# Modulation of four early chunks by row sums on VectorE, and a first group of four feature tiles as two groups of two

## The chip, the cores and the metric

The kernel runs on one core of one Trainium2 chip. The metric is device time in microseconds (us), the median of several runs of the whole program. All arrays are fp32 in HBM. To keep fp32 accuracy, the large products split each operand into a high part (rounded to the matmul's type, fp32r) and a low part (the rest), and sum three products: high x high, high x low, low x high.

## The reference, cut to what matters

One layer of an encoder, with 256 tokens and 2048 features. The conditioning vector c yields six vectors of 2048 (shift, scale and gate for each of two sub-layers). The change touches only the first shift and scale and the QKV projection that uses them.

```python
c_act = jax.nn.silu(c)
mod = c_act @ mod_w[i] + mod_b[i]
sh_m, sc_m, g_m, sh_f, sc_f, g_f = jnp.split(mod, 6, axis=-1)
hmix = x * (1.0 + sc_m[:, None, :]) + sh_m[:, None, :]
y = windowed_gqa_sink(hmix, positions, w_qkv, b_qkv, sink, w_o, b_o)   # proj = h @ w_qkv + b_qkv, width 3072
x = layer_norm(alpha * x + (1.0 + g_m[:, None, :]) * y, ln_mix_g[i], ln_mix_b[i])
hff = x * (1.0 + sc_f[:, None, :]) + sh_f[:, None, :]
y = sq_relu_mlp(hff, w1, b1, w2, b2)                                   # 2048 -> 8192 -> 2048
x = layer_norm(alpha * x + (1.0 + g_f[:, None, :]) * y, ln_mlp_g[i], ln_mlp_b[i])
```

## The kernel before

**Feature tiles and groups.** The 2048 features are 16 tiles of 128 (k = 0 to 15). QKV needs all of them as its contraction. The kernel cannot touch tile k before its shift and scale are known, and these are sums over all 2048 entries of c. So it takes the tiles in groups (`MIXG`, L32): 1, 1, 2, 4, 4, 4. For each group it streams the columns of `mod_w` that yield the group's scale and shift (array `modm`, two chunks for each tile), and then the rows of `w_qkv` for those tiles. Everything comes in chunks of 1 MiB, [128, 2048] fp32.

**The stream.** Class `Stream` (L174) holds the order of all chunks in `S.q`, as `plan` put them there. `loads` (L196) issues a load on the SP queue (L202) whenever one of the raw buffers is free: five, and three more (`MORE`) in the early part, out of memory that later serves as `gen2`. Entries of `S.side` are extra loads (parts of x) at fixed places of the order. `pump` (L223) goes through the chunks in this order. A weight chunk is cast in two halves to its high part on ScalarE (L247), and `low` (L214) makes the low part on VectorE (L218). A modulation chunk calls its `step`, if the pump was allowed that many (`vecs`); otherwise the pump stops there. The pump is called at the start of each weight chunk (`main`, L253) and after each half of it (`done`, L264), with `S.pace` modulation steps at most. While `S.pin` is set, what it issues keeps its place in its engine's program order; otherwise the tile framework may place it. With `S.behind`, a step's first matmul is put behind the latest matmul of the main work.

**Modulation.** Class `Mod` (L285): for most chunks `step` makes 16 small products on TensorE, c as a 32-wide stationary operand and the chunk as moving operand, four side by side (`quad`, L304; L307), accumulated in PSUM over the whole group. For listed chunks (`dve`) it multiplies by c on VectorE instead (L343 for the first, L345 after) into a partial sum that a last product folds in. Then the sum is copied to a row (L361), and `columns` (L365) turns the row into one value per partition through TensorE (L370, L377), and adds bias and 1 (L371 to L384). `modulated(g)` (L512) applies scale and shift to each tile of the group: high part on ScalarE (L519), product and low part on VectorE (L520, L521).

**QKV.** Output channels are six blocks of 512 (c). `qkv_first` (L542) does tiles 0 and 1, `qkv` (L563) the other groups, one weight chunk at a time: four (k, c) blocks, two token tiles, three products (`mm3`, L498 to L500), so 24 matmuls of 512 columns. `evict` (L526) then adds the two PSUM banks of a channel to its running sum on VectorE (L537), or copies them the first time on ScalarE (L535) after the bias product (L163). A pair in `CARRY` leaves its channel in PSUM for the next group. `ORDER` gives the order of a group's chunks; the six chunks in `LATE` are left for the attention stage. After the first chunk of the last group comes the rotary work (`rope`, L648 to L651), then attention, its projection, and the MLP.

**Start.** While the first chunks load, `idle(n)` (L597) keeps TensorE running with products of ones (L601).

## Time and profile before

| | us |
|---|---|
| median of 3 runs | 1095.23 |
| lowest, highest | 1093.78, 1096.64 |
| span of the profiled execution | 1098.2 |

The profiled execution is on record by its span alone, from its first instruction to its last. Engines: PE is TensorE's matmuls, PEld its weight loads, DVE VectorE, ACT ScalarE, POOL GpSimd, SP the engine that issues most loads. Busy shares over the span are 97% PE, 73% DVE, 48% ACT. A busy PE is not PE at its peak, since matmuls are pipelined and their ends are modelled. "L218" is line 218 of the kernel. In a row of a timeline or of the chain of waits, the first number is the start and the second the length. In a group's row stand the count, the total busy time, the mean in ns, and the idle time ahead of it with what ended it.

### The profile page before, as it was taken

What the parts mean: (1) busy time and instruction counts of PE and PEld (TensorE: products, weight loads), DVE (VectorE), ACT (ScalarE), POOL (GpSimd) and SP (SyncE); (2) the same over time, 40 slices, a digit from 0 to 9 for tenths busy, and PEclk for the clock granted to TensorE, in tenths of its full rate; (3) what the DMA queues carried; (4) which work ended last, traced back from release to release, by engine and by line L of the source; (5) the groups of instructions that cost most, each with busy time, mean ns of one, the idle gap of its engine ahead of it and who ended that gap; (6) DMA issues with size and microseconds to landing.
All of it is one profiled execution on the core that took longest, in us unless ns stands there. A gap on an engine that the chain in (4) does not pass through costs nothing.

```text
span 1098.2 us, 15487 instructions
## 1 busy us (share of the span) xinstructions
PE 1067.6 (97%) x6098; PEld 863.1 (79%) x6098; DVE 804.2 (73%) x1162; ACT 522.0 (48%) x806; POOL 30.0 (3%) x54
## 2 busy tenths in 40 slices
PE   8889999998999999999999999999999999999995
PEld 6657677665677799988888888888888888888884
DVE  4597899978899877754588889756666557665676
ACT  5333346765673537643344543344453334544340
POOL 1000000001000000000000010001000000000001
PEclk9989999999999999999999999999999999999998
DMA  9999987789985996555578788866555555557511
GB/s 384 425 427 425 427 357 280 271 297 379 377 315 201 361 360 244 185 192 192 195 301 303 272 313 306 312 220 225 184 189 190 197 196 186 178 185 267 191 75 77
DMA packets 43337, 292.70 MB, mean 267 GB/s; under 512 B 5104, under 2 KB 5232, under 8 KB 9472
## 3 DMA queue, kind: packets, MB, share of 16 engines
q1 hardware_dynamic: 39312, 279.85, 66.9%
q0 software_dynamic: 3200, 10.50, 2.7%
q10 hardware_dynamic: 752, 1.35, 0.3%
q8 instruction: 48, 0.79, 0.3%
q14 instruction: 25, 0.20, 0.0%
HBM read 289.57 MB, written 2.11 MB: 266 GB/s over the span
## 4 chain that ended last, share of the span: by engine, by line
PE 86%; DVE 7%; DMA 4%; ACT 2%; issue 1%; DVEq 0%; ACTq 0%
PE pa L995 16%; PE pa L500 15%; PE pa L498 15%; PE pa L499 15%; PE pa L996 8%; PE pa L972 3%; PE pa L971 3%; PE pa L973 3%; PE pm L307 3%; DVE wl L218 2%; DMA raw<-in_modm 2%; DMA raw<-in_modf 1%; DVE g L345 1%; DMA raw<-in_wqkv 1%; PE pa L687 1%; PE pa L743 1%
## 5 line engine op out<-in xcount | busy, mean ns | idle before, releaser
L218 DVE TENSOR_TENSOR wl<-raw,wh 128x1024 fp32r<-128x1024 f32 x332 | 403.9, 1223 | 223.6 <-ACT wh L247 222.9
L247 ACT CAST wh<-raw 128x1024 fp32r<-128x1024 f32 x332 | 347.1, 1051 | 441.3 <-PE pa L500 228.6
L498 PE MATMUL pa<-wh,g 128*128 128x512 f32 x816 | 324.1, 398 | 5.1 <-ACT g L519 2.6
L500 PE MATMUL pa<-wh,g 128*128 128x512 f32 x816 | 318.9, 392 | 4.1 <-DVE g L521 3.0
L499 PE MATMUL pa<-wl,g 128*128 128x512 f32 x816 | 320.0, 392 | 0.0
L995 PE MATMUL pa<-g,wh 128*128 128x512 f32 x768 | 270.1, 397 | 0.0
L996 PE MATMUL pa<-g,wl 128*128 128x256 f32 x768 | 214.9, 280 | 0.0
L498 PEld LDWEIGHTS pa<-wh,g 128*128 128x128 f32 x816 | 153.9, 189 | 46.8 <-issue 7.5
L500 PEld LDWEIGHTS pa<-wh,g 128*128 128x128 f32 x816 | 153.5, 188 | 41.2 <-DVE g L521 6.0
L499 PEld LDWEIGHTS pa<-wl,g 128*128 128x128 f32 x816 | 153.9, 189 | 33.0 <-issue 2.4
L995 PEld LDWEIGHTS pa<-g,wh 128*128 128x128 f32 x768 | 144.2, 188 | 36.0 <-issue 0.8
L996 PEld LDWEIGHTS pa<-g,wl 128*128 128x128 f32 x768 | 144.8, 189 | 0.1
L345 DVE SCALAR_TENSOR_TENSOR g<-raw,cact,g 128x1024 f32<-128x1024 f32 x65 | 82.6, 1280 | 2.8 <-DMA raw<-in_modf 2.3
L972 PE MATMUL pa<-g,wh 128*128 128x256 f32 x256 | 72.7, 285 | 0.4 <-DVE g L915 0.4
L971 PE MATMUL pa<-g,wh 128*128 128x256 f32 x256 | 72.5, 286 | 0.0
L973 PE MATMUL pa<-g,wl 128*128 128x256 f32 x256 | 72.3, 283 | 0.0
L307 PE MATMUL pm<-raw,cact 128*32 128x256 f32 (+2 forms) x776 | 48.8, 375 | 5.9 <-DMA raw<-in_modf 3.2
L971 PEld LDWEIGHTS pa<-g,wh 128*128 128x128 f32 x256 | 48.8, 192 | 1.3 <-issue 0.8
L972 PEld LDWEIGHTS pa<-g,wh 128*128 128x128 f32 x256 | 49.1, 192 | 0.9 <-DVE g L915 0.8
L973 PEld LDWEIGHTS pa<-g,wl 128*128 128x128 f32 x256 | 49.1, 192 | 0.0
L345 DVE SCALAR_TENSOR_TENSOR g4b<-raw,cact,g4b 128x1024 f32<-128x1024 f32 x32 | 40.7, 1280 | 9.0 <-DMA raw<-in_modgf 8.8
L307 PEld LDWEIGHTS pm<-raw,cact 128*32 128x32 f32 x776 | 20.9, 112 | 25.9 <-issue 11.5
(165 smaller groups left out, 741.6 us busy)
## 6 DMA issues: line engine op xcount, KB each, us to landing
raw<-in_w SPq DMA_DIRECT2D x64, 1024.0 KB, 4.9
raw<-in_w1b SPq DMA_DIRECT2D x48, 1024.0 KB, 5.0
raw<-in_modm SPq DMA_DIRECT2D x32, 1024.0 KB, 14.8
raw<-in_modf SPq DMA_DIRECT2D x32, 1024.0 KB, 6.9
raw<-in_wqkv SPq DMA_DIRECT2D x24, 1024.0 KB, 12.8
raw<-in_modgm SPq DMA_DIRECT2D x16, 1024.0 KB, 7.5
raw<-in_wo SPq DMA_DIRECT2D x16, 1024.0 KB, 7.5
raw<-in_w1a SPq DMA_DIRECT2D x16, 1024.0 KB, 7.6
```

Of the source, the lines that this page charges most:

```text
L218: self.pinned(nc.vector.tensor_sub(l, r, f32(self.hs[n])))
L247: self.pinned(nc.scalar.copy(h, s))
L307: i = nc.tensor.matmul(self.ps[32 * j:32 * j + 32, :w], lhsT[j] if type(lhsT) is list else lhsT, rhs[j], start=self.first, stop=stop)
L345: nc.vector.scalar_tensor_tensor(p[:, :e], s, cact[:, kt:kt + 1], p[:, :e], op0=OP.mult, op1=OP.add)
L498: nc.tensor.matmul(ps, xh, wh, start=start, stop=False)
L499: nc.tensor.matmul(ps, xh, wl, start=False, stop=False)
L500: S.prev = nc.tensor.matmul(ps, xl, wh, start=False, stop=stop).ins
L971: nc.tensor.matmul(o, wh(w, 128), hh, start=new, stop=False)
L972: nc.tensor.matmul(o, wh(w, 128), hl, start=False, stop=False)
L973: nc.tensor.matmul(o, wl(w, 128), hh, start=False, stop=end)
L995: nc.tensor.matmul(ps, wh(k, 128), hb, start=k == 0, stop=False)
L996: nc.tensor.matmul(ps[:, :256], wl(k, 128), hb[:, :256], start=False, stop=k == NK - 1)
```

## The change

1. `MIXG` becomes 1, 1, 2, 2, 2, 4, 4: tiles 4 to 7 are two groups of two, with eight modulation chunks in all as before, all of them now on TensorE (before, four of the eight on VectorE), and six weight chunks.
2. `MIXM` describes a new layout of `modm`: tiles 0 and 3 keep a pair of chunks for TensorE (`pair`), tiles 1 and 2 have a chunk with the 128 scale columns and one with the 128 shift columns, transposed, so that each partition holds one output feature and its 2048 weights. Class `Col` sums such a chunk along its row on VectorE, times c, with one `tensor_tensor_reduce` that starts from the bias. For that `broadcast_c` puts c into all partitions once (16 products and four copies on ScalarE).
3. `modulated` can take the tiles of a group one by one (used for tiles 2 and 3).
4. The planned order of chunks (`MODAT`), the carried channels and the place of the loads of x are set anew.
5. `S.steps` overrides the pace at single points; `STEPS` gives it for tiles 2 to 7 with `S.behind` set, and the steps of tiles 0 to 3 are called at named points of `run`. `ahead(nh)` casts up to nh halves in advance.
6. The fillers at the start become 7, 5 and 14 (before 16, 5 and 6).
7. The scratch tiles "t2" move from the small pool to a pool of their own that takes the memory of c's broadcast copy later.

```diff
-MIXG = (1, 1, 2, 4, 4, 4)
+MIXG = (1, 1, 2, 2, 2, 4, 4)
+MIXM = (1, 0, 0, 1, 2, 2, 4, 4)
...
+    cbp = early.enter_context(tc.tile_pool(name="cbp", bufs=1))
...
+            more.append(ctx.enter_context(tc.tile_pool(name="t2p", bufs=4)))
...
-            self.pump(self.pace, 2 * i + 2)
+            self.pump(self.steps.pop(0) if self.steps else self.pace, 2 * i + 2)
...
-                self.pump(self.pace)
+                self.pump(self.steps.pop(0) if self.steps else self.pace)
...
+    class Col:
+        def __init__(self, src, n, k):
+            self.src, self.n, self.k = src, n, k
+
+        def plan(self):
+            S.plan(self.src, self.step)
+
+        def step(self, raw):
+            d = (scm, shm)[self.n][:, self.k:self.k + 1]
+            S.pinned(nc.vector.tensor_tensor_reduce(out=raw, in0=raw, in1=cb, scale=1.0,
+                                                    scalar=modmb[:, self.n, self.k:self.k + 1],
+                                                    op0=OP.mult, op1=OP.add, accum_out=d))
+            if self.n == 0:
+                S.pinned(nc.vector.tensor_scalar_add(d, d, 1.0))
+
+    def broadcast_c():
+
+        cb = cbp.tile([128, D], F32, name="cb")
+        for q in range(4):
+            ps = psa.tile([128, 512], F32, name="pa")
+            for i in range(4):
+                nc.tensor.matmul(ps[:, i * 128:i * 128 + 128],
+                                 cact[:, 4 * q + i:4 * q + i + 1].to_broadcast([128, 128]), ident,
+                                 start=i == 0, stop=i == 3)
+            nc.scalar.copy(cb[:, q * 512:q * 512 + 512], ps)
+        return cb
...
-    m_mix = groups(a["modm"], MIXG, [(), (), (), (1, 3, 4, 6), (1, 3, 4, 6), (1, 3, 4, 6)])
+    pair = {k: Mod([a["modm"][2 * k + i] for i in range(2)], 64) for k in (0, 3)}
+    col = {(n, k): Col(a["modm"][2 * k + n], n, k) for n in range(2) for k in (1, 2)}
+    m_mix = [(pair[0], 0, 1), (None, 1, 1), (pair[3], 2, 2)]
+    m_mix += [(m, k0 + 4, nk) for m, k0, nk in groups(a["modm"][8:], MIXG[3:],
+                                                      [(), (), (1, 3, 4, 6), (1, 3, 4, 6)])]
...
-    LATE = [(4, 3), (5, 3), (4, 4), (5, 4), (4, 5), (5, 5)]
-
-    ORDER = {2: (1, 0, 2), 3: (5, 4, 3, 0, 2, 1), 4: (1, 2, 0), 5: (0, 1, 2)}
-    CARRY = {(LATE[n], LATE[n][1]) for n in (0, 2, 4)} | {((2, 2), 5), ((3, 1), 1), ((4, 0), 0), ((1, 2), 2)}
+    LATE = [(5, 3), (6, 3), (5, 4), (6, 4), (5, 5), (6, 5)]
+
+    ORDER = {2: (1, 0, 2), 3: (2, 0, 1), 4: (1, 2, 0), 5: (1, 2, 0), 6: (0, 1, 2)}
+    CARRY = {(LATE[n], LATE[n][1]) for n in (0, 2, 4)} | {((2, 2), 5), ((3, 1), 3), ((4, 0), 1), ((5, 0), 0), ((1, 2), 2)}
...
     m_mix[0][0].plan(2)
     S.plan(a["wqkv"][0])
-    m_mix[1][0].plan(2)
+    col[0, 1].plan()
+    col[1, 1].plan()
     S.plan(a["wqkv"][1])
+    S.side[len(S.q)] = lambda: load_x(1)
+    col[0, 2].plan()
     S.plan(a["wqkv"][2])
-
-    S.side[len(S.q)] = lambda: load_x(1)
-    m_mix[2][0].plan(3)
+    col[1, 2].plan()
+    pair[3].plan(2)
     wq(2, 1)
-    m_mix[2][0].plan(1)
+    MODAT = {2: (0, 4, 0), 3: (1, 2, 1), 4: (3, 3, 2), 5: (4, 4, 0)}
     for g in range(2, G):
-        n = len(ORDER[g])
-        if g + 1 < G:
-            S.side[len(S.q)] = lambda g=g: load_x(g)
-        for x, c in enumerate(ORDER[g][1:], 1):
+        if g > 3 and g + 1 < G:
+            S.side[len(S.q)] = lambda g=g: load_x(g - 1)
+        for x, c in enumerate(ORDER[g][1:]):
             if g + 1 < G:
-                m_mix[g + 1][0].plan([0, 0, 3][x] if g == 2 else [0, 2, 2, 2, 1, 1][x] if n == 6 else [0, 4, 4][x])
+                m_mix[g + 1][0].plan(MODAT[g][x])
             wq(g, c)
         if g == 2:
-            m_mix[3][0].plan(4)
+            S.side[len(S.q)] = lambda: load_x(2)
         if g + 1 < G:
+            m_mix[g + 1][0].plan(MODAT[g][2])
             wq(g + 1, ORDER[g + 1][0])
-        if g == 2:
-            m_mix[3][0].plan(1)
...
-    def modulated(g):
+    def modulated(g, ks=None):
         m, k0, nk = m_mix[g]
-        columns(m, modmb, (scm, shm), k0, nk)
-        hh, hl = g4(F32R), g4(F32R)
-        for k in range(nk):
+        ks = range(nk) if ks is None else ks
+        if m is not None and (k0 > 3 or k0 + ks[-1] in pair):
+            columns(m, modmb, (scm, shm), *((k0, nk) if k0 > 3 else (k0 + ks[-1], 1)))
+        if g not in held:
+            held[g] = g4(F32R), g4(F32R)
+        hh, hl = held[g]
+        for k in ks:
...
+    def ahead(nh):
+
+        S.nh = nh
+        S.pump(0)
+        S.nh = 5
+
     load_x(0)
     bq = bias_rows(a["bqkv"], QKV)
-    idle(16)
+    idle(7)
+    cb = broadcast_c()
     S.pin = True
     S.vecs(1)
     idle(5)
     S.vecs(1)
     modulated(0)
-    idle(6)
+    idle(14)
     msk = masks()
     S.nh, S.nl = 5, 4
-    S.pace = 1
-    run(qkv_first(0))
-    S.vecs(2)
-    run(qkv_first(1), [lambda: modulated(1)])
+    S.pace = 0
+    run(qkv_first(0), [lambda: S.vecs(2), lambda: ahead(2)])
+    run(qkv_first(1), [lambda: modulated(1), lambda: S.vecs(1), lambda: ahead(5)])
     trig = rotary_tables()
-    run(qkv_first(2))
-    S.vecs(4)
-    modulated(2)
+    run(qkv_first(2, [lambda: S.vecs(1)]), [lambda: S.vecs(1)])
+    modulated(2, [0])
+    S.vecs(1)
+    ahead(1)
+    modulated(2, [1])
     S.pace = VECS
+    STEPS = {(2, 1): (0, 0, 1), (2, 0): (0, 1, 1), (2, 2): (1, 0, 0),
+             (3, 2): (0, 1, 0), (3, 0): (0, 1, 1), (3, 1): (1, 0, 0)}
     S.pin = False
     for x, (g, c) in enumerate(qk_order):
         at = ORDER[g].index(c)
         mid = []
         if g < G - 1 and at == len(ORDER[g]) - 1:
             mid.append(lambda: modulated(g + 1))
+        S.steps = list(STEPS.get((g, c), ()))
+        S.behind = (g, c) in STEPS
         run(qkv(g, c), mid)
```

More of the change, by code (lines that the diff above doesn't have):

```diff
@@ L191, in __init__ @@
             self.side = {}
+            self.steps = []
         def plan(self, src, use=None, kept=0):
@@ L540, in banks, with qkv_first @@
         return [psa.tile([128, 512], F32, name="pa") for _ in range(NT)]
-    def qkv_first(n):
+    def qkv_first(n, then=()):
         wh, wl = S.main()
+        for f in then:
+            f()
         for i, (g, p) in enumerate(FIRST[n]):
@@ L1030, in hybrid_kernel @@
             if blk == 1:
-                gb = [sml.tile([128, 512], F32, name="gb", tag="t2", bufs=4) for _ in range(2)]
+                gb = [t2("gb") for _ in range(2)]
                 for n in range(2):
```

27 lines of the change are left out of this document (16 added, 11 removed).

## The prediction

> **What bounds the kernel now.** I began with the stretches of the span, because an average over 1098 us would hide that this kernel has stages with different limits.
>
> ```profile
> core 0: us, PE busy (x) PEld busy (x) DVE busy (x) ACT busy (x) POOL busy (x), PEclk, DMA share, GB/s
> 0.00:12.00 12.00, 9.95 (x88) 7.47 (x88) 5.31 (x20) 5.46 (x9) 4.96 (x16) 1.00 0.85 332
> 12.00:50.00 38.00, 32.82 (x319) 23.47 (x318) 17.42 (x28) 19.84 (x30) 0.00 (x0) 0.96 1.01 425
> 50.00:73.00 23.00, 21.77 (x134) 14.60 (x130) 22.96 (x31) 3.98 (x6) 1.01 (x2) 1.00 1.01 426
> 73.00:111.00 38.00, 35.61 (x183) 26.56 (x183) 29.04 (x36) 14.24 (x17) 0.90 (x1) 0.91 1.01 427
> 111.00:149.00 38.00, 35.56 (x208) 24.61 (x207) 32.92 (x48) 14.67 (x20) 0.00 (x0) 1.00 1.01 425
> 149.00:260.00 111.00, 109.75 (x605) 75.13 (x604) 101.98 (x195) 73.02 (x172) 4.25 (x8) 1.00 0.77 295
> 260.00:400.00 140.00, 136.34 (x938) 102.48 (x937) 121.71 (x231) 83.30 (x173) 3.96 (x6) 1.00 0.83 323
> 400.00:1098.00 698.00, 685.83 (x3639) 588.75 (x3637) 472.81 (x579) 307.49 (x384) 14.87 (x22) 0.99 0.60 218
> ```
>
> The row is: stretch, busy time of each engine with its instructions, granted clock, DMA share, rate. From 12 to 149 us the transfers never rest (share 1.01, 425 GB/s), so one 1 MiB chunk lands every 1.0486/0.426 = 2.46 us and no edit can bring data sooner. From 149 to 260 us the rate falls to 295 GB/s and VectorE is busy 102 of 111 us; after 400 us TensorE is busy 98%. Whatever the front gains or loses is therefore handed on to the end: behind it no transfer is short.
>
> TensorE's busy share says little in the front, so I counted matmuls. One 1 MiB chunk of QKV weights is four (k, c) blocks by two token tiles, hence 8 of the L500 kind (and 24 in all).
>
> ```profile
> 0.00:50.00 50.00, 9.53 (x24) 4.57 (x24) 0.97 0.97 402
> 50.00:73.00 23.00, 9.36 (x24) 4.48 (x24) 1.00 1.01 426
> 73.00:111.00 38.00, 16.83 (x43) 8.32 (x42) 0.91 1.01 427
> 111.00:149.00 38.00, 15.53 (x41) 7.36 (x41) 1.00 1.01 425
> ```
>
> By 73 us TensorE has done 48/8 = 6 chunks; eight have landed (counted below). Then come 43/8 = 5.4 chunks in 38 us. The chain of waits (start, length, what) says which limit acts when:
>
> ```profile
> 11.93 18.74 DMA raw<-in_modm
> ...
> 58.76 14.05 DMA raw<-in_wqkv
> 73.86 1.04 ACT wh L247
> 74.89 0.51 ACT g L519
> 75.45 0.79 PE pa L498
> ...
> 78.84 0.43 PE pa L500
> ...
> 82.79 0.23 PE pa L499
> ...
> 103.77 1.43 PE pm L307 x24
> ...
> 110.61 2.35 DVE wl L218 x2
> ...
> 129.13 1.48 PE pm L307 x24
> ...
> 130.90 0.87 ACT wh L247
> ...
> 134.84 1.22 DVE wl L218
> ...
> 139.12 2.36 DVE wl L218 x2
> ...
> 142.32 0.50 PE pa L500
> ```
>
> No transfer stands on the chain after 72.81 us. From 75 to 110 us it is TensorE working off the six chunks of feature tiles 4 to 7, which could not start before all eight modulation chunks of that group were in; then VectorE and ScalarE catch up with what had piled up. The first visible limit after the front is VectorE's rotary work:
>
> ```profile
> 66.66 0.61 PE L307 MATMUL pm<-g,onesf 128*32 128x256 f32 x8
> 148.50 0.69 DVE L537 TENSOR_TENSOR g<-g,pa 128x512 f32<-128x512 f32 x1 [0.68 <-PE pa L500]
> 149.22 0.69 DVE L648 TENSOR_TENSOR g<-g,trig 128x512 f32<-128x512 f32 x1
> ```
>
> **When chunks land.** The two DMA pieces of the chain end at 30.67 us (the tenth chunk, 10.25 MiB of the planned order with 0.25 of x) and at 72.81 us (27.25 MiB: the second weight chunk of the group of four): 42.14/17 = 2.48 us per MiB, which agrees with the rate. Counting on at 2.46 us, the last modulation chunk lands at 72.8 + 20.5 x 2.46 = 123.2 us, the third weight chunk of tiles 8 to 11 at 125.7, the first of tiles 12 to 15 at 128.1. TensorE takes that last modulation chunk only at 129.13: the front runs some 6 us behind its transfers.
>
> **The change, part by part.** From the first weight chunk of tiles 8 to 11 (38.25 MiB, 99.9 us) on, the planned order is the same as before, byte for byte. So the only thing to be won is the lateness.
>
> *Group of four as two groups.* In the new order the modulation of tiles 4, 5 is complete at 48.2 us (17.25 MiB), its weight chunks land at 54.4, 59.3 and 66.7; tiles 6, 7 are complete at 69.1, weights at 71.6, 82.6, 92.5; the last chunk of tiles 2, 3 lands ahead of them at 50.7. A chunk is 24 x 0.23 = 5.5 us of TensorE and begins about 2.6 us after landing (72.81 to 75.45). So tiles 2, 3 end at 50.7 + 2.6 + 5.5 = 58.8, and the six chunks run 58.8 to 64.3, to 69.8, to 75.3, to 80.8, then 85.2 to 90.7 and 95.1 to 100.6. The backlog is gone at about 101 us where it was worked off at 110.6. Tiles 8 to 11 then start when their last modulation chunk (97.4 us) has gone through, near 107 us, not after 118.
>
> *Price on VectorE.* The kinds that matter:
>
> ```profile
> L345 DVE SCALAR_TENSOR_TENSOR g<-raw,cact,g 128x1024 f32<-128x1024 f32 x65 | 82.6, 1280 | 2.8 <-DMA raw<-in_modf 2.3
> L343 DVE TENSOR_SCALAR g<-raw,cact 128x1024 f32<-128x1024 f32 x7 | 5.3, 751 | 4.1 <-DMA raw<-in_modm 4.0
> L537 DVE TENSOR_TENSOR g<-g,pa 128x512 f32<-128x512 f32 x42 | 27.7, 684 | 10.3 <-PE pa L500 10.2
> L693 DVE CUSTOM_DVE_ANT_0 pa<-pa,msk,nsnk 128x256 f32<-128x256 f32 x64 | 27.2, 488 | 0.2 <-PE pa L687 0.2
> L693 DVE DVE_READ_ACCUMULATOR2_ANT nm<- 128x1 f32 x64 | 9.1, 142 | 0.0
> ```
>
> Before, four of the group's eight chunks were VectorE's: 2 x 0.75 + 6 x 1.28 = 9.2 us, now TensorE's. There are seven groups, not six, so six more channel evictions, less one more that is carried in PSUM: 5 x 2 x 0.684 = +6.8 us. The four row sums are the L693 kind, eight times as long. L345 adds 1280 - 751 = 0.53 us per step over its single-source neighbour and still runs 1024 elements in 1.28 us, so by elements alone a row sum is 2 x 1.28 + 0.14 = 2.7 us; by eight times L693 it is 3.9 + 0.14 = 4.0. I take 2.7, the row of equal operand kind (two sources in SBUF); 10.8 us for four, at most 16. They fall into 14 to 30 us, and VectorE is busy there only 17.4 of 38 us: with 16 it still fits. From 50 to 111 us VectorE sheds 9.2 and gains 6.8. Net on the path: 0; without that cover it would be the +6.8.
>
> [...]
>
> *TensorE.* Four chunks fewer by row sums and four more from the group of four: even. The broadcast of c is 16 products in place of nine fillers:
>
> ```profile
> 1.57 6.32 PE L601 MATMUL pa<-onesr 128*128 128x512 f32 x16 [1.57 <-DVE onesr L92]
> 11.95 1.63 PE L601 MATMUL pa<-onesr 128*128 128x512 f32 x6
> 159.66 0.87 PE pt L667 x8
> ```
>
> (The first two rows are from the timeline, the third from the chain.) A filler costs 6.32/16 = 0.40, nine are 3.6 us. A 128-wide fp32 product is 0.87/8 = 0.11 as one pass and twice that as two: 1.7 to 3.5 us. Eight more late fillers are 8 x 0.27 = 2.2 us, from about 13.6 to 15.8 us, with the first real matmul due near 15.4: 0 to 0.4 us, absorbed by the wait for the next weight chunk. Four more ScalarE copies in 5 to 11 us lie in its idle half (5.46 of 12 us busy). The renamed scratch pool moves no work.
>
> *Steps by hand.* In the first 50 us and in tiles 2 to 7, a modulation step is issued at a named point, behind the matmuls of the chunk in hand. Behind such a step on TensorE's queue stand the next chunk's matmuls, so each waits for its landing; going through the order, every step stands at or after its landing (for instance the four chunks of tiles 4, 5 land at 40.8 to 48.2, and their steps stand behind matmuls that run from 44 to 53 by the same count). I cost this at 0. What it can cost is in the last rival. On the SP queue the load of x for tiles 4 to 7 now stands behind the third weight chunk of tiles 2, 3, not ahead of the second: same bytes, and 8 us ahead of its use.
>
> *The end of the front.* The last weight chunk before the rotary work lands at 128.1. By TensorE: 125.7 + 2.6 + 5.5 + 5.5 = 139.3, and two evictions, 1.4: 140.7. By modulation: 123.2, a step of 1.0 us, then from that step to the first matmul 8.8 us (66.66 to 75.45, tiles 4 to 7) or 13.2 (129.13 to 142.32, tiles 12 to 15), 5.5 and 1.4: 139.9 to 144.3. The later path counts: 140.7 to 144.3 against 149.22, a gain of 4.9 to 8.5 us. I take 6: nearer the slow row, as those are the same tiles in the same order, but part of their 13.2 us was catching up (casts and splits from 130.90 to 141.5). Sum: 1098.2 - 6 = 1092.2 for the profiled execution, whose only time on record is its span. It stands 3.0 us over the median of the runs, so **1095.2 - 6 = 1089.2**.
>
> **Rivals.** (a) *More than that.* The half-clock stretches vanish too (0.96 in 12 to 50, 0.91 in 73 to 111; matmuls 0.43 us apart at 78.84, 0.23 at 82.79), and VectorE reaches 149 us with spare splits done: 3 to 6 us more, 1084. Against it: the landing bound above holds for everything before 141.
>
> (b) *No change.* With the backlog gone TensorE has work for three chunks (16.5 us) between 101 and 128 us; it waits two or three times for some 5 us. Waits of that kind before 75 us ended in matmuls at half clock until past 81: about 3.4 us lost. Two of these, and the gain is gone: 1095. For it: that row; against: from 111 to 149 us there were waits as well, at clock 1.00. [...]
>
> (c) *Slower: the stream of transfers gets holes.* There are eight early buffers.
>
> ```profile
> raw<-in_modm SPq DMA_DIRECT2D x32, 1024.0 KB, 14.8
> ```
>
> A load takes 14.8 us from issue to landing, nearly all of it queueing behind others; eight buffers are 8 x 2.46 = 19.7 us of stream, so a chunk may stay some 17 us after landing (19.7 less its own transfer) before the queue runs dry. With the pace at zero a chunk that the hand-placed list leaves for later blocks every chunk behind it from being cast and freed. If several chunks wait 20 us and more, each microsecond without transfers before 128 us is one at the end: 12 to 18 us of holes, less the 6, give 1101 to 1107. For it: SP already waits for buffers on most loads; against: by the landings above no step waits over 5 us.
>
> **How the numbers follow.** Forecast, 1087 to 1091: 0.52. (a) 1080 to 1086: 0.13. (b) 1092 to 1098: 0.15. (c) and like cases above 1098.5: 0.20. A change under 0.3% (3.3 us) can't be told from none here. So faster 0.65, same 0.15, slower 0.20. The range leaves out about 0.05 below and 0.12 above: 1082 to 1101; the forecast's own is 1087 to 1091.
>
> **What would show it.** Right: matmuls of tiles 4, 5 at about 59 us, when no chunk of tiles 2, 3 is left; six chunks of tiles 4 to 7 done by 101 to 104; a DMA piece (123 to 128 us landing) back on the chain; rotary work from 141 to 144; everything after shifted alike. Row sums of 2.7 us or less in 14 to 30 us. Wrong: DMA share under 1 anywhere from 12 to 128 us (c), a clock under 1 from 100 to 130 (b), rotary work at 149 or later, or a shift at 149 that is gone by 400 us.

## The result and the profile after

| | median us | lowest to highest | runs |
|---|---|---|---|
| before | 1096.1 | 1093.78 to 1101.0 | 20 |
| after | 1099.82 | 1096.28 to 1102.42 | 20 |

The ratio is 1.0026 (95% interval 1.0015 to 1.0036): the change makes the kernel slower by 1.6 to 3.9 us. Forecast were 6 us the other way. By the 0.3% named in the prediction this lies at the edge of no change; it is told from none by its interval.

The profiled execution of after has a span of 1094.5 us and took 1096.28 us, so 1.78 us lie around the span; it was the shortest of its 20. The profile of before (span 1098.2) is at the long end of its runs. The two spans must therefore not be set against each other; stages are compared, and other profiles of both kernels stand in for the usual run. The stretches of after, with the columns of the prediction's first fence:

```profile
12.00:50.00 38.00, 36.05 (x259) 28.00 (x254) 31.36 (x44) 18.55 (x28) 0.00 (x0) 1.00 1.01 426
50.00:73.00 23.00, 22.45 (x233) 17.18 (x229) 16.46 (x24) 9.04 (x11) 0.95 (x1) 1.00 1.01 425
73.00:111.00 38.00, 34.55 (x267) 23.69 (x267) 29.39 (x41) 8.72 (x12) 0.96 (x1) 1.00 0.99 404
111.00:149.00 38.00, 31.80 (x178) 22.16 (x170) 32.93 (x45) 15.53 (x21) 0.00 (x0) 0.91 1.01 426
```

To 73 us it came as hoped: TensorE is busier (36.05 and 22.45 us against 32.82 and 21.77) at full clock, the transfers never rest. From 73 us the transfers have holes (404 GB/s against 427), and from 111 us TensorE stands still for 6 of 38 us and loses clock (31.80 us at 0.91 against 35.56 at 1.00). The timeline of after gives the start of the rotary work (L703 was L648):

```profile
123.14 0.50 PE L538 MATMUL pa<-wh,g 128*128 128x512 f32 x1 [0.17 <-DVE g L563]
149.04 0.69 DVE L703 TENSOR_TENSOR g<-g,trig 128x512 f32<-128x512 f32 x1
```

149.04 against 149.22: the front gained 0.18 us, and lost more in the usual run (next section). The first row is the first product with a low part of tiles 8 to 11. Before, the same one (L500) started at 123.31:

```profile
123.31 0.50 PE L500 MATMUL pa<-wh,g 128*128 128x512 f32 x1 [2.23 <-DVE g L521]
```

From there to the rotary work after and before take 25.90 and 25.91 us.

Behind the front the profiles show no effect of the change. The span less the start of the rotary work is 945.5 us in the three profiles of after. In the two profiles of before it is 949.0 and 949.9: from 257 us VectorE, ScalarE and TensorE waited for late transfers, up to 3.53 us at a time, where after's profiles show at most 0.73 us. This does not go with the kernel: `b_w_sooner` below, the kernel before with one edit, has 945.8, and `m5_on_pe` and `w_sooner`, edits of after, have 949.5 and 950.2. The first of the waits in before:

```profile
256.83 1.28 DVE L345 SCALAR_TENSOR_TENSOR g<-raw,cact,g 128x1024 f32<-128x1024 f32 x1 [2.33 <-DMA raw<-in_modf]
```

So the profile of before has the longer span although its kernel has the shorter median. With 945.5 in place of 949.0, its 149.22 would make a run of 149.22 + 945.5 + 1.78 = 1096.5 us, which is its median. By the same sum the median of after, 1099.8, has its rotary work near 152.5 us.

### The profile page after: what moved, and what is told of

Same layout as the page of the kernel before. It is cut to its first block, busy times and chain, and to the rows that moved or that the text cites. A ratio compares the mean times of both kernels' runs of the same rounds, so it can differ in the third digit from the quotient of the medians.

```text
span 1094.5 us, 15675 instructions
## 1 busy us (share of the span) xinstructions
PE 1066.7 (97%) x6184; PEld 866.0 (79%) x6184; DVE 811.4 (74%) x1174; ACT 523.5 (48%) x810; POOL 30.4 (3%) x54
## 4 chain that ended last, share of the span: by engine, by line
PE 87%; DVE 8%; ACT 2%; DMA 1%; issue 1%; DVEq 0%; ACTq 0%
PE pa L1050 16%; PE pa L538 16%; PE pa L536 15%; PE pa L537 15%; PE pa L1051 8%; PE pa L1027 3%; PE pa L1026 3%; PE pa L1028 3%; PE pm L314 3%; DVE wl L225 2%; DVE g L352 2%; ACT wh L254 1%; PE pa L742 1%; DMA raw<-in_wqkv 1%; PE pa L798 1%; DVE pa L748 1%
## 5 line engine op out<-in xcount | busy, mean ns | idle before, releaser
L352 DVE SCALAR_TENSOR_TENSOR g<-raw,cact,g 128x1024 f32<-128x1024 f32 x58 | 73.6, 1279 | 1.1 <-DMA raw<-in_modf 0.7
L578 DVE TENSOR_TENSOR g<-g,pa 128x512 f32<-128x512 f32 x52 | 34.6, 683 | 18.8 <-PE pa L538 18.7
L352 DVE SCALAR_TENSOR_TENSOR g4b<-raw,cact,g4b 128x1024 f32<-128x1024 f32 x32 | 40.7, 1279 | 10.0 <-DMA raw<-in_modgf 10.0
L314 PE MATMUL pm<-raw,cact 128*32 128x128 f32 (+2 forms) x840 | 47.0, 350 | 1.1 <-DMA raw<-in_modf 1.1
```

The lines of the kernel that those rows point to most:

```text
L314: i = nc.tensor.matmul(self.ps[32 * j:32 * j + 32, :w], lhsT[j] if type(lhsT) is list else lhsT, rhs[j], start=self.first, stop=stop)
L352: nc.vector.scalar_tensor_tensor(p[:, :e], s, cact[:, kt:kt + 1], p[:, :e], op0=OP.mult, op1=OP.add)
```

## The experiments

Five sets of kernels, each against the kernel before on the same chip (medians 1095.8, 1096.18, 1096.07, 1095.95 and 1095.95 us). "R" is the start of the rotary work, "L" the start of the first product with a low part of tiles 8 to 11, both in the profile. Up to R, half clock lasted 3.41 us (from 30.60 us) and 6.83 us (from 74.98) in the profile of before, and 6.83 us (from 115.37) in that of after.

### Both kernels once more

`before_again`, `after_again`, `after_third`: no edit.

> The kernel before, unchanged, for a second profile and more runs. Theory A (half-clock stretches in the front make the runs of one kernel differ): spans follow the mean granted clock of the run, about 3.4 us for each 0.0031 (one stretch of 6.83 us at half clock). Theory B (a wait for a transfer at 250 to 265 us, which the two profiles show 3.5 us apart, makes them differ): spans differ by about 3.5 us at equal clock, and this profile's front (rotary work at 149.2) is unchanged.

> The changed kernel, unchanged, for a second profile and more runs: median 1098 to 1101. Theory A: this profile has two half-clock stretches between 95 and 135 us and its rotary work starts 2 to 4 us later than 149.0. Theory B: rotary work at 149.0 again, and the difference to the first profile appears at 250 to 265 us.

> The change as it is, a control on the same chip as the three runs beside it. In 26 runs of it so far the mean granted clock was 0.990, so (1 - clock) x span was 10.3 to 11.5 us, and time less that product 1089.0 to 1089.3 us; for the kernel before 6.7 to 7.6 and 1089.3 to 1089.9 us. Clock theory (the change is slower because TensorE is granted half clock more often in the front, and for nothing else): 1099 to 1101 us, clock 0.990 within 0.001, time less the product 1089 to 1090 us again. Rival (the work itself takes longer): time less the product 1092 us or more.

| | median us | ratio (95%) | L | R |
|---|---|---|---|---|
| before_again | 1096.83 | 1.0014 (1.0002 to 1.0025) | 121.69 | 149.22 |
| after_again | 1100.50 | 1.0045 (1.0029 to 1.006) | 126.93 | 152.84 |
| after_third | 1099.28 | 1.0021 (1.0007 to 1.0034) | 124.72 | 150.66 |

The kernel before starts its rotary work at the same moment in both profiles, after at 149.04, 150.66 and 152.84: what varies in after is L, and R follows it by 25.9 us. In `before_again` L came 1.6 us sooner than in before and R did not: half clock from 123.2 to 126.6 us, behind L, took the time back. So before's front ended unchanged, as theory B had it, and after's 3.8 us later with two stretches of half clock, as theory A had it. In `after_again` the stretch from 73 us shows the holes more plainly, and half clock ahead of 111 us as well:

```profile
73.00:111.00 38.00, 34.55 (x255) 24.40 (x254) 30.52 (x40) 7.14 (x9) 0.95 (x1) 0.96 0.97 382
```

These holes begin before 92 us, and in `after_again` (first and third row; the second is of after) half clock had come early, from 41 to 44.5 us:

```profile
12.00:50.00 38.00, 36.05 (x259) 28.21 (x259) 30.81 (x42) 18.43 (x28) 0.00 (x0) 0.96 1.01 425
73.00:92.00 19.00, 19.00 (x162) 13.35 (x158) 12.57 (x20) 5.15 (x7) 0.96 (x1) 1.00 1.01 427
73.00:92.00 19.00, 19.00 (x175) 13.73 (x174) 12.04 (x21) 5.14 (x7) 0.95 (x1) 1.00 1.00 396
```

The two go together in every profile of after and its edits that has the hand-placed steps: the five with half clock in 12 to 50 us move 383 to 397 GB/s from 73 to 92 us, the eleven without it 426 or 427, and ScalarE begins to cast the last weight chunk of tiles 6, 7 at 94.37 us in `after_again` against 92.49 in after. How the one leads to the other was not followed.

The mean granted clock of 20 runs of after was 0.991, that of 33 runs of before 0.994. Time less (1 - clock) x span came out as 1089.2 and 1089.5 us. So the loss goes with the clock; whether the clock is its cause was tried below.

### Parts of the change undone

`col_on_pe`: the row sums undone, tiles 0 to 3 in pairs for TensorE.

```diff
-MIXM = (1, 0, 0, 1, 2, 2, 4, 4)
+MIXM = (1, 1, 1, 1, 2, 2, 4, 4)
...
-    idle(7)
-    cb = broadcast_c()
+    idle(16)
```

> The changed kernel without the row sums: tiles 1 and 2 use pairs of chunks on TensorE like tiles 0 and 3, without the broadcast of c and with 16 fillers at the start as before. Theory H (the row sums hold VectorE in the first 35 us and delay the start of tiles 1 to 3): time 1 to 4 us less than the changed kernel's. Rival (the front is set behind 85 us, whatever the first 35 us do): rotary work and time within 1.5 us of the changed kernel's; TensorE waits for the steps of tiles 1 and 2 early and catches up by 85 us.

1100.29 us, ratio 1.0029 (1.0017 to 1.0042), L 126.83, R 152.72: as after itself. The row sums show neither gain nor loss, as the rival had it.

`steps_undone`: the table of hand-placed steps emptied.

```diff
-    STEPS = {(2, 1): (0, 0, 1), (2, 0): (0, 1, 1), (2, 2): (1, 0, 0),
-             (3, 2): (0, 1, 0), (3, 0): (0, 1, 1), (3, 1): (1, 0, 0)}
+    STEPS = {}
```

> The change without its table of early steps placed by hand (tiles 2-5 get their steps by the pace of VectorE chunks, as in the kernel before; the split group and the row sums stay). If the hand-placed steps cost nothing and gain nothing: 1099 to 1102 us, rotary work at 149 to 153 us. If they are what made the front lose its gain: 1094 to 1097 us and a transfer share of 1.00 or more in 73 to 111 us. If they protect the front: 1103 us or more.

1098.55 us, ratio 1.0023 (1.0012 to 1.0034), L 125.25, R 151.18. Its stretches:

```profile
73.00:111.00 38.00, 31.70 (x188) 21.50 (x191) 29.89 (x38) 10.22 (x13) 0.95 (x1) 0.91 1.01 426
111.00:149.00 38.00, 36.75 (x211) 26.17 (x204) 33.44 (x50) 15.09 (x20) 0.00 (x0) 1.00 1.01 423
```

The transfers have no holes now, so the hand-placed steps are needed for them; they are not enough, as `no_rows` below keeps the steps and has none either (426 GB/s). But the wait and the half clock have only moved ahead of 111 us, and R is no earlier. The steps alone are not what ate the gain.

### The order of two steps on ScalarE

In after, the casts of tiles 8 to 11's second weight chunk stand on ScalarE ahead of the scaled inputs (L561) that TensorE waits for. `mod5_first` takes the modulation of tiles 8 to 11 early enough to put L561 first; `mod56_first` does so for tiles 12 to 15 as well.

```diff
-        S.steps = list(STEPS.get((g, c), ()))
+        S.steps = list({**STEPS, **{(4, 1): (1, 1, 1), (4, 2): (1, 1, 1), (4, 0): (2, 0, 2)}}.get((g, c), ()))
...
+        if (g, c) in ((4, 0),):
+            S.nh = 3
+            mid.append(lambda: setattr(S, "nh", 5))
```

> The changed kernel, with the scale and shift of tiles 8 to 11 ahead of the casts of their second weight chunk on ScalarE, and ahead of the next group's row sums on VectorE. Theory C (the expected gain went into this order: ScalarE waits 3.7 us for that chunk's transfer with the modulation queued behind it): the first matmul on tiles 8 to 11 comes at 113 to 116 us, not after 118, with their low part done by 117 and not 125; rotary work 2 to 5 us earlier than 149.0, time 2 to 5 us less than the changed kernel's. Theory D (the last transfers set the end of the front): rotary work within 1 us of 149.0, time unchanged.

> As the run before, and the same rule for the last group (tiles 12 to 15): no modulation step of a later group and no cast beyond the next half chunk ahead of its scale and shift. Theory C: 1 to 3 us less again than with tiles 8 to 11 alone. Theory D: unchanged.

1107.24 us (ratio 1.0109, 1.0095 to 1.0124) and 1104.88 us (1.0078, 1.0065 to 1.0091): the worst of all. The order came out as meant, L561 at 112.72 and 111.68 us, L at 115.10 and 114.21, and the first products of tiles 8 to 11 came at 113.37 and 112.33, as theory C had it. But R is 156.82 and 154.97, which neither theory had. The stretch from 111 us of `mod5_first`:

```profile
111.00:149.00 38.00, 28.77 (x152) 18.48 (x152) 28.17 (x39) 13.99 (x20) 0.00 (x0) 0.87 0.96 389
```

VectorE reached the row work of the last group later (its first piece at 117.32 us against 113.05), the transfers fell to 389 GB/s, and TensorE waited more; that the row work held the buffers is inferred. That order alone is refuted as the cause.

### Row work moved to TensorE

In each group of four, VectorE takes four of eight chunks (L350, L352). `m5_on_pe` gives those of tiles 8 to 11 to TensorE, `m56_on_pe` those of tiles 8 to 15 (its edit is shown).

```diff
-                                                      [(), (), (1, 3, 4, 6), (1, 3, 4, 6)])]
+                                                      [(), (), (), ()])]
```

> The changed kernel with all eight modulation chunks of tiles 8 to 11 on TensorE (none on VectorE). Theory E (VectorE's in-order queue from 89 to 111 us holds both the buffers, so that transfers pause, and the low parts TensorE waits for): VectorE loses 9.2 us there, the DMA share of 80 to 125 us is 1.0 again, the first chunk of the last group lands at 125.5 rather than 127.5 to 129.9, rotary work at 143 to 147 us, time 3 to 7 us less than the changed kernel's. Rival F (the wait is for the transfers themselves, or TensorE's clock alone): rotary work within 1.5 us of 149 to 153, time within 1.5 us of the changed kernel's.

> As the run before, and the same for tiles 12 to 15: VectorE loses another 9.2 us between 112 and 130 us, TensorE gains 4 us. Theory E: rotary work another 1 to 4 us earlier. Rival F: no earlier, or later by TensorE's extra work.

1098.75 us (ratio 1.0023, 1.0011 to 1.0034), L 126.46, R 152.31; and 1098.16 us (1.0017, 0.9996 to 1.0038), L 121.95, R 151.10. Theory E's R of 143 to 147 us did not come. Both are within the noise of after, whose three ratios are 1.0021 to 1.0045: what VectorE loses, TensorE has to do, and from 73 to 111 us it is now busy all 38 us (34.55 in after). Time less (1 - clock) x span rose to 1091.8 and 1091.1.

### The place of one weight chunk

`w_sooner`, `w_sooner_m56` (with `m56_on_pe`), and the kernel before with the same edit, `b_w_sooner`:

```diff
-    MODAT = {2: (0, 4, 0), 3: (1, 2, 1), 4: (3, 3, 2), 5: (4, 4, 0)}
+    MODAT = {2: (0, 4, 0), 3: (1, 2, 1), 4: (3, 3, 2), 5: (1, 7, 0)}
```

> The change, with the second weight chunk of tiles 8-11 three places earlier in the stream of transfers (behind one chunk of the last group's modulation, not behind four). In the profile of the change that chunk landed at 115.33 us; its casts on ScalarE stood ahead of the scaled inputs of tiles 8-11 (117.41 us), and TensorE stood still for 5.81 us at 112.1 us, with half clock right behind it (115.37 to 122.20 us). Late-chunk theory: the chunk lands near 108 us, the first scaled input of tiles 8-11 is made by 113 us, the wait of 5.81 us is under 2 us, at most one half-clock stretch is left in 100 to 125 us, the rotary work starts at 144 to 148 us, and the time is 1094 to 1097 us. VectorE theory (its order of row work, splits and evictions sets the front, and every earlier demand on it holds buffers longer, as in the two runs that took the modulation of tiles 8-11 first): the transfers' share falls under 0.98 in 100 to 125 us, the rotary work starts at 152 to 157 us, 1102 to 1107 us.

> The same earlier place of that weight chunk, and the modulation chunks that VectorE still takes for tiles 8-15 (four of eight in each group) given to TensorE. With the chunks alone moved to TensorE the median was 1098.16 us, the rotary work started at 151.10 us in a profile with two half-clock stretches before it. Late-chunk theory: 1092 to 1096 us. VectorE theory: VectorE has some 5 us more in 85 to 125 us, so it is better than the earlier chunk alone by 4 us or more. If transfers alone bound the front: 1096 to 1099 us, rotary work at 149 to 151 us, whatever VectorE and the weights do.

> The kernel before the change, with the second weight chunk of tiles 8-11 three places earlier in the stream, all else as it was: the control for the two runs above. Its backlog of tiles 4-7 keeps TensorE at work to about 118 us, so an earlier chunk has at most the wait of 2.23 us at 121.1 us to win. Late-chunk theory: 1094 to 1097 us, rotary work at 147 to 149.3 us. If an earlier weight chunk itself upsets buffers and VectorE's order: 1099 us or more.

| | median us | ratio (95%) | L | R |
|---|---|---|---|---|
| w_sooner | 1101.68 | 1.0057 (1.0037 to 1.0078) | 118.19 | 152.66 |
| w_sooner_m56 | 1098.91 | 1.0035 (1.0018 to 1.0052) | 115.73 | 150.98 |
| b_w_sooner | 1097.72 | 1.0015 (1.0000 to 1.0031) | 115.50 | 148.04 |

The chunk landed at 107 us, TensorE began on tiles 8 to 11 3.6 us sooner than in after, and then waited for VectorE in other places. TensorE's waits from 85 to 157 us in `w_sooner` (total, count, longest):

```profile
PE pa L537 <- DVE wl L225: 3.5, 2, 2.4
PE pa L536 <- ACT g L561: 2.8, 1, 2.8
PE pa L538 <- DVE g L563: 2.6, 1, 2.6
PE pm L314 <- DVE g L352: 2.3, 1, 2.3
```

In `w_sooner` both theories missed in part: R was in VectorE's range, but the transfers kept share 1.00 (413 GB/s) from 100 to 125 us. `w_sooner_m56` came out as its third theory, transfers alone, had it. `b_w_sooner` had the R of its late-chunk theory and a time 0.7 us above it.

`b_w_sooner` also shows how far L can be trusted. L came 7.8 us sooner than in the kernel before and R only 1.2 us, though TensorE waited no more than 2.7 us in all from 85 to 157 us: the rest was TensorE's own work, with half clock from 133 to 136 us. So R follows L by 25.9 us where L is late, as in after; once L comes early, what stands behind it sets R.

### The clock as a cause

`keep_warm` puts 16 products of ones ahead of the last weight chunk of tiles 6, 7 and 16 behind the modulation of tiles 8 to 11. `fill24` puts 24 right where TensorE stood still at 112 us, in a PSUM bank that nothing waits for, tied into the order; `fill24_8` (its edit is shown) adds 8 ahead of the wait of 2.43 us at 101 us.

```diff
             pss = half.pop(c, None) or banks()
+            if ci == 0:
+                warm({(5, 1): 24, (4, 0): 8}.get((g, ch), 0))
...
+    def warm(n):
+        if n:
+            ps = pst.tile([128, 512], F32, name="pt")
+        for j in range(n):
+            i = nc.tensor.matmul(ps, onesr, onesr[:, None, :].to_broadcast([128, 4, 128]), start=True, stop=True)
+            behind(i, fence.pop() if fence else S.prev)
+            fence.append(i.ins)
```

> The changed kernel with two lots of 16 filler products on TensorE where it waits, ahead of the last weight chunk of tiles 6 and 7 and behind the modulation of tiles 8 to 11. Theory G (the loss against the kernel before is the half-clock stretches from 100 to 130 us): most runs have a mean clock of 0.993 to 0.995 in place of 0.989 to 0.990, and the time is 2 to 5 us less than the changed kernel's. Rival (the clock falls while nothing waits for TensorE): clock up, time unchanged or up to 2 us more, the fillers' own delay.

> The change, with 24 matmuls on constants (24 x 0.23 = 5.5 us) put into TensorE's queue between the last matmul of tiles 6-7 and the first of tiles 8-11, the place where it stood still for 5.81 us at 112.1 us. Nothing else in the order of TensorE moves. Clock theory: the two half-clock stretches behind that wait (115.37 to 122.20 us) are gone, (1 - clock) x span falls by 3 to 4 us to 7 to 8 us, the rotary work starts 1.5 to 3 us sooner than in the control beside it, the time is 1095.5 to 1098 us. Rival (half clock comes wherever it comes, or is set by the rest of the front): clock as in the control, time as in the control or up to 3 us more, as the fillers hold up the first matmuls of tiles 8-11.

> The same, with 8 more matmuls on constants (1.8 us) ahead of the last weight chunk of tiles 6-7, where TensorE waited 2.43 us for the low part of the weights at 101.1 us (in a second profile of the change a half-clock stretch began at 106.24 us). Clock theory: another 0 to 1.7 us less than with the 24 alone, 1094 to 1097 us. Rival: as the control, or 2 to 4 us more than it for the matmuls that do no work.

| | median us | ratio (95%) | mean clock | L | R |
|---|---|---|---|---|---|
| keep_warm | 1103.16 | 1.0063 (1.0043 to 1.0083) | 0.991 | 124.21 | 154.00 |
| fill24 | 1100.08 | 1.0041 (1.0025 to 1.0057) | 0.993 | 124.37 | 151.80 |
| fill24_8 | 1098.69 | 1.0019 (1.0005 to 1.0032) | 0.995 | 125.45 | 151.36 |
| after_third, beside the last two | 1099.28 | 1.0021 (1.0007 to 1.0034) | 0.991 | 124.72 | 150.66 |

`keep_warm` moved more than it added: the last step of tiles 8 to 11's modulation came ahead of the last chunk's products in TensorE's queue and waited 6.39 us for VectorE's row work (L352), with half clock from 104.8 us; it tells nothing of the clock. `fill24_8` did what it should for the clock:

```profile
73.00:111.00 38.00, 36.37 (x282) 25.64 (x284) 30.58 (x40) 7.14 (x9) 0.96 (x1) 1.00 0.97 381
111.00:149.00 38.00, 35.46 (x220) 24.68 (x209) 32.08 (x46) 16.48 (x22) 0.00 (x0) 1.00 1.01 426
```

TensorE keeps full clock from 73 to 149 us, and the median is 0.6 us under the control's, inside both intervals. Mean (1 - clock) x span fell to 5.1 from 10.2 us, and time less that product rose to 1093.1 from 1088.6. The fillers held nothing up here: behind the eight TensorE still waited 0.63 us, behind the 24 still 0.38 us. So the clock theory, with 1094 to 1097 us, did not come true, though `after_third` itself came near what it said of the control (1088.6 us less that product, 1089 to 1090 expected).

The traces say why half clock can be free. In after it lies from 115.37 to 122.20 us, where TensorE has to wait for VectorE's low part (L) anyway. It is not always free: in `after_again` the stretch from 106 us stands on the chain of waits, and 3.4 us at half clock cost an estimated 1.7, half their length. And the test has a limit: its profile had half clock in 12 to 50 us, and the last chunk of tiles 6, 7 was late (cast at 94.29 us) ahead of all the fillers, as in `after_again`, against which its R is 1.5 us sooner. Half clock from 100 to 130 us is thus not the whole of the loss; what it costs in the usual run is open.

### Row work left out

`no_rows` takes the work away without giving it to anyone:

```diff
                     new = self.part is None
+                    if not new and self in few:
+                        continue
...
+    few.extend(m for m, _, nk in m_mix if nk == 4)
```

`no_rows_w` adds the edit of `w_sooner`, `no_rows_first` that of `mod5_first`.

> The change, with the row work of VectorE for the modulation of tiles 8-11 and 12-15 left out but for its first piece: 14 of 16 pieces, 7 x 1.2 = 8.4 us for each group, are not computed by any engine, and their buffers come free at once. VectorE theory (its queue from 89 to 123 us and the buffers that it holds set the end of the front): the transfers' share is 1.01 in 73 to 125 us, the rotary work starts at 141 to 146 us and the time is 1089 to 1094 us. TensorE and transfer theory (the front ends a fixed work of TensorE, some 31 us, behind the first matmul of tiles 8-11, which waits for the stream of transfers): the first matmul of tiles 8-11 not before 114 us, the rotary work at 146 to 150 us, 1094 to 1098 us.

> The change without VectorE's row work for tiles 8-15 (14 of 16 pieces computed by no engine, as in the run before), and with the second weight chunk of tiles 8-11 three places earlier in the stream. Without the row work the transfers ran at full share, that chunk landed at 113.5 us and the rotary work began at 147.46 us. Joint theory (the place of that chunk and VectorE's queue both hold the front; either alone moves nothing): the chunk lands near 106 us, the first scaled input of tiles 8-11 is made by 110 us, the rotary work starts at 139 to 144 us, the time is 1087 to 1092 us. Rival (TensorE's own work, or a later transfer, holds the end): rotary work at 146 to 149 us, 1094 to 1097 us.

> The change without that row work, and with the modulation of tiles 8-11 ahead of the casts of that weight chunk (the edit that with the row work in place put the rotary work at 156.82 us). Joint theory: VectorE's queue was what that edit ran into, so without the row work it gains: first scaled input of tiles 8-11 by 110 us, rotary work at 139 to 145 us, 1087 to 1092 us. Rival: the edit is bad in itself (held buffers, half clock), rotary work at 149 us or later, 1097 us or more.

| | median us | ratio (95%) | L | R |
|---|---|---|---|---|
| no_rows | 1096.49 | 0.9998 (0.9985 to 1.001) | 117.94 | 147.46 |
| no_rows_w | 1094.03 | 0.9973 (0.996 to 0.9987) | 115.24 | 146.99 |
| no_rows_first | 1091.05 | 0.9947 (0.993 to 0.9964) | 109.26 | 141.58 |

`no_rows` came out as TensorE and transfer theory had it: with the row work gone and the transfers at share 1.01, the chunk still landed only at 113.6 us, ScalarE cast it ahead of the scaled inputs, and TensorE waited 6.45 us. The other two were to show whether that chunk's place and VectorE's queue hold the front together. Against `after_third` beside it, `no_rows` takes 2.8 us less. The sooner chunk gave 0.5 us of R more, as the rival had it. The other order of steps did what the joint theory said: with the row work in place its R is 7.8 us later than in the profile of after, without the row work 5.9 us sooner than in `no_rows` and 7.5 us sooner than in after. Its ScalarE, its TensorE, the rotary work and its last stretch:

```profile
106.88 2.08 ACT L565 ACTIVATE g<-g,shm,scm 128x256 fp32r<-128x256 f32 x4
113.15 2.00 ACT L254 CAST wh<-raw 128x1024 fp32r<-128x1024 f32 x2 [4.20 <-DMA raw<-in_wqkv]
109.26 0.50 PE L542 MATMUL pa<-wh,g 128*128 128x512 f32 x1 [0.54 <-DVE g L567]
141.58 0.69 DVE L710 TENSOR_TENSOR g<-g,trig 128x512 f32<-128x512 f32 x1
111.00:149.00 38.00, 36.22 (x206) 24.86 (x200) 27.72 (x39) 15.41 (x18) 0.00 (x0) 1.00 1.01 426
```

The scaled inputs (L565 here) now stand ahead of the casts that wait for the chunk; from 73 us on there is no half clock and no hole. The forecast's 141 to 144 us exist, but only for a kernel that leaves VectorE's row work out. Whether the row work given to TensorE, together with this order, keeps part of it was not tried. No version that computes everything beat the kernel before.

## Why the prediction was wrong, point by point

**The start from the profile.** The prediction set the span of 1098.2 against the median of run times and took that execution for 3.0 us above it. As 1.78 us lie around a span, it was some 4.8 us above, and 3.5 us of that lay behind the front. The forecast of 6 us does not rest on it.

**The floor: right as far as it was reached.** By transfers and TensorE the rotary work could begin at 140.7. `no_rows_first`, without the row work and without holes, began it at 141.58.

**The row sums: right.** The groups of after:

```profile
L381 DVE CUSTOM_DVE_ANT_0 raw<-raw,cb,pack 128x2048 f32<-128x2048 f32 x4 | 9.4, 2345 | 0.0
L578 DVE TENSOR_TENSOR g<-g,pa 128x512 f32<-128x512 f32 x52 | 34.6, 683 | 18.8 <-PE pa L538 18.7
```

2345 ns and some 82 ns for the accumulator's read: 2.43 us for one, forecast 2.7, 9.7 us for four. With two fp32 sources and an accumulator this instruction runs 2048 elements in 2.35 us, as L345 runs 1024 in 1.28: the count by elements held, and the 4.0 us by eight times L693 did not come. The 16 products that broadcast c are 32 matmul records, two for each, and took 4.41 us from 4.73 us on, where the prediction had 1.7 to 3.5. The ten more evictions came too (52 for 42).

**The backlog: right in kind, late in size.** The forecast worked it off at 101 us, against 110.6. Measured by the last low product of tiles 4 to 7, it ended at about 110.0, against 116.9 before: 7 us sooner, not 10. Tiles 4, 5 began as counted (their scaled inputs, L561, at 58.85), but those of tiles 6, 7 came at 82.76, where the count has TensorE begin at 75.3: 5.5 us for each chunk left out TensorE's modulation products, 7.2 us from 50 to 85 us. The last weight chunk landed as counted (ScalarE cast it at 92.49 us), but the term "begins about 2.6 us after landing" was 11 us for its low part. VectorE and TensorE of after:

```profile
92.85 2.35 DVE L225 TENSOR_TENSOR wl<-raw,wh 128x1024 fp32r<-128x1024 f32 x2
95.12 1.28 DVE L352 SCALAR_TENSOR_TENSOR g<-raw,cact,g 128x1024 f32<-128x1024 f32 x1
...
100.50 1.27 DVE L352 SCALAR_TENSOR_TENSOR g<-raw,cact,g 128x1024 f32<-128x1024 f32 x1
101.70 0.68 DVE L578 TENSOR_TENSOR g<-g,pa 128x512 f32<-128x512 f32 x1
102.30 2.35 DVE L225 TENSOR_TENSOR wl<-raw,wh 128x1024 fp32r<-128x1024 f32 x2
...
103.56 0.50 PE L537 MATMUL pa<-wl,g 128*128 128x512 f32 x1 [2.43 <-DVE wl L225]
```

Row work for the next group's modulation, each piece followed by an eviction, stood ahead of the splits, and TensorE waited for them.

**"Tiles 8 to 11 then start ... near 107 us, not after 118": the step that failed.** It took the lateness of 6 us behind the transfers for TensorE's backlog alone, and let TensorE begin as soon as the modulation was through. TensorE began on them at 117.96, and could go on with their low parts at 123.14, as before. ScalarE, TensorE and VectorE of after:

```profile
109.42 0.37 ACT L368 COPY mrow<-pm 128x256 f32<-128x256 f32 x1 [14.94 <-PE pm L314]
109.69 1.99 ACT L254 CAST wh<-raw 128x1024 fp32r<-128x1024 f32 x2
115.42 1.99 ACT L254 CAST wh<-raw 128x1024 fp32r<-128x1024 f32 x2 [3.73 <-DMA raw<-in_wqkv]
117.31 2.07 ACT L561 ACTIVATE g<-g,shm,scm 128x256 fp32r<-128x256 f32 x4
117.96 0.79 PE L536 MATMUL pa<-wh,g 128*128 128x512 f32 x1 [5.81 <-ACT g L561]
110.52 0.17 DVE L418 TENSOR_SCALAR scm<-scm 128x4 f32<-128x4 f32 x1
110.77 2.36 DVE L225 TENSOR_TENSOR wl<-raw,wh 128x1024 fp32r<-128x1024 f32 x2
113.05 0.75 DVE L350 TENSOR_SCALAR g<-raw,cact 128x1024 f32<-128x1024 f32 x1
113.84 3.93 DVE L352 SCALAR_TENSOR_TENSOR g<-raw,cact,g 128x1024 f32<-128x1024 f32 x3
117.68 2.35 DVE L225 TENSOR_TENSOR wl<-raw,wh 128x1024 fp32r<-128x1024 f32 x2
...
122.67 0.42 DVE L563 TENSOR_TENSOR g<-g,g 128x256 fp32r<-128x256 f32 x1
```

The scale is ready at 110.52. ScalarE stands 14.94 us for the modulation row; then comes one weight chunk, 3.73 us of waiting for the next, and only then L561: TensorE waits 5.81 us. By the prediction's own rate that next chunk lands five chunks behind the first, at 99.9 + 5 x 2.46 = 112.2 us, already past 107; it landed at 115.34. VectorE does splits, four pieces of the last group's row work and the splits of that next chunk before the low parts. Now the kernel before, whose VectorE did this:

```profile
113.22 0.75 DVE L343 TENSOR_SCALAR g<-raw,cact 128x1024 f32<-128x1024 f32 x1
114.00 3.92 DVE L345 SCALAR_TENSOR_TENSOR g<-raw,cact,g 128x1024 f32<-128x1024 f32 x3
117.85 2.35 DVE L218 TENSOR_TENSOR wl<-raw,wh 128x1024 fp32r<-128x1024 f32 x2
...
122.83 0.42 DVE L521 TENSOR_TENSOR g<-g,g 128x256 fp32r<-128x256 f32 x1
```

It is the same queue, 0.17 us apart. The backlog covered it; without the backlog it is bare. The chain of waits of after runs through all three engines:

```profile
102.38 2.28 DVE wl L225 x2
...
104.67 10.66 DMA raw<-in_wqkv
...
115.42 1.99 ACT wh L254 x2
117.41 0.51 ACT g L561
...
128.97 1.48 PE pm L314 x24
...
142.15 0.50 PE pa L538
```

The split that ends at 104.66 stands behind VectorE's row work; it is followed by the load of the next chunk, then come that chunk's casts and only then the scaled inputs. In the sum, the term that failed is "By modulation: 123.2, a step of 1.0 us": TensorE came to the last modulation chunk at 128.97 (129.13 before). Behind it the slow row's 13.2 us (128.97 to 142.15), 5.5 and 1.4 came as counted and give 149.1. "From the first weight chunk on the order is the same" was true, and was the reason for no gain, not for one.

**"Net on the path: 0" for VectorE: wrong with it.** The busy shares counted free time in a stretch; what mattered was which instruction stands ahead of which. In after's chain the row work of tiles 8 to 15 stands from 90 to 102 and from 120 to 123 us; between them stand the chunk's load and its casts.

**The rivals.** (b) came as a mechanism, not as a price: TensorE waited, and had half clock for 6.83 us from 115.37 us.

```profile
111.00:115.37 4.37, 1.15 (x24) 0.41 (x15) 4.30 (x5) 0.69 (x1) 0.00 (x0) 1.00 1.02 427
115.37:122.20 6.83, 4.24 (x16) 2.78 (x20) 6.79 (x7) 3.97 (x6) 0.00 (x0) 0.50 1.00 423
```

Half clock began inside the wait of 5.81 us (112.15 to 117.96 us). It came with shorter waits too: behind one of 2.43 us (last section) and, in before, inside one of 2.39 us (73.06 to 75.45 us), with half clock from 74.98 to 81.80 us: the 3.4 us lost in the prediction's 0.91 row. But (b)'s price, "two of these, and the gain is gone", was not how it went: in after half clock fell where TensorE waited for VectorE anyway, and `fill24_8` without half clock from 73 us on is no faster. (c) came in a small form: share 0.99 in this profile, 0.97 in `after_again`, with 404 and 382 GB/s. Against 427 GB/s these are 38 x (1 - 404/427) = 2.0 us and 4.0 us of transfers lost; R moved by 3.8 us between the two, the holes by 2.0. They come in two parts: ahead of 92 us with early half clock and the hand-placed steps, behind it only in kernels that have both those steps and the row work of tiles 8 to 15, as after does. They are not the whole, as R is 151.18 without the steps.

**The steps by hand at 0: about right.** Without them the median is 1098.55, against 1099.3 to 1100.5 for after; the ratios to before overlap (1.0023 against 1.0021 to 1.0045).

What stays open is the share of each in the 3 to 4 us by which the usual run of after is slower: holes, VectorE's order and half clock vary together from run to run. In after's three profiles their common place is shown, the front up to the first low parts of tiles 8 to 11.

## What to carry to other kernels

When a backlog goes, ask for each engine what its next instruction waits for, before the time is booked as won: the queue that the backlog covered was as long as the backlog. A stretch in which an engine is 77% busy (VectorE in after, 29.39 of 38 us from 73 us on) can still set the end, if the one result that the others wait for stands last in it. And an edit that loses alone can win once another limit is gone (here the order of steps: 7.8 us later with the row work, 5.9 us sooner without it): leave work out altogether to see which engine holds the time, since moving it to another engine (`m56_on_pe`) filled that one, 27.00 of 27 us from 73 us on, and left R at 151.10.

## What the runs showed of the hardware

The same wait did not always cost the clock. TensorE waited 2.43 us at 101.1 us in after and in `after_third`; after went on at full clock to 115.37 us, `after_third` was at half from 105.0:

```profile
101.00:105.00 4.00, 1.57 (x7) 1.24 (x7) 4.00 (x5) 0.00 (x0) 0.00 (x0) 1.00 0.94 340
105.00:108.40 3.40, 3.40 (x9) 2.67 (x8) 3.20 (x4) 0.00 (x0) 0.00 (x0) 0.50 1.00 407
```

The two rows are of `after_third`. So a wait of 2.43 us can be followed by half clock or not; `fill24` and `after_again` have the same wait, with half clock from 104.1 and 106.2 us. The three profiles of after differ by 3.80 us in R (149.04 to 152.84).
